# Modulation matmuls in groups of eight k tiles, and their sums turned into columns by transposes and a vector sum

## The chip, the cores and the metric

The kernel runs on one core of a Trainium2 chip. The metric is device time in microseconds (us), lower is better. It was 1266.31 us in the median of three runs (1264.38, 1266.31 and 1266.55).

## What is computed

The reference is one step of a two-layer transformer trunk on 128 context tokens and 256 latent tokens, each 2048 wide. Each layer normalizes its input and modulates it by shift, scale and gate, which are products of a condition vector with a weight matrix of 2048 x 6144:

```python
def modulate(x, cond, norm_w, ada_w, ada_b):
    m = jax.nn.silu(cond) @ ada_w + ada_b
    shift, scale, gate = jnp.split(m, 3, axis=-1)
    h = rmsnorm(x, norm_w) * (1 + scale[:, None]) + shift[:, None]
    return h, gate[:, None]
```

There are two conditions, one for the context tokens and one for the latent tokens. After the modulation, layer 0 projects h to queries, keys, values, pooling inputs and gates, runs differential attention and a pooling mixer, and projects back. Layer 1 does the same with grouped-query attention. Everything is float32. The change touches only how m is computed and handed on.

## The kernel before

All large products are 3-term products: activations and weights are each split into a high and a low part, and each tile product is three matmuls (L428, L429 and L430 of `mm3`). A weight tile is loaded by SyncE (SP) into a buffer `raw` (two buffers of 512 KB), ScalarE (ACT) makes its high part `wh` (L404), and VectorE (DVE) its low part `wl` (L406). TensorE (PE) then runs the matmuls into the PSUM tiles `mm`.

The modulation of layer 0 stands ahead of the first projections. Its shift and scale are made in nine groups of output columns (`GROUPS`): two groups of one block of 128 columns, then seven of two blocks. One group is handled by `ada_group`. For shift and then for scale it walks the 16 k tiles of the weights. Each k tile is one matmul (L486), in which the two conditions, padded to 32 columns (`cond_cols`), are the stationary operand and the weight columns are moving; with 256 columns moving, the kernel calls it 32x256. The output goes to 32 partitions of one PSUM tile, and four consecutive k tiles go to four different sets of 32 partitions, so the tile ends with four partial sums for each condition. Each float32 matmul of this kind is two records in the trace.

One item of the work list covers four k tiles. Its loads bring four k tiles of 128 columns in one transfer, or two of 256 columns, or one of 512 columns, 256 KB each, in 11 buffers named `aw` (seven) and `acc` (four). When all 16 k tiles of shift and scale are summed, ACT copies the PSUM tile to `kq` (L490), and `mod` turns rows into columns: for each block of 128 columns a matmul with the constant `sel` (L506) adds the four partial sums and leaves two columns. `set_shift` and `set_scale` (L517 and L520, on DVE) read them from PSUM and fill the tile `AB`. `make_h` then makes the modulated tiles h of that group (L291 on DVE, L294 on ACT, L296 on DVE), and the query and key projections that use these tiles can follow. A segment of the projections is listed one group after the group that completes its h tiles.

Three more groups of this kind belong to layer 1: s0 and s3 (shift) and h0 (gate). Each has 512 columns, 16 loads of 256 KB, and the first two end in `mod` too. h0 runs at the boundary between the layers, where PE also transposes the last block of x (L258) and multiplies with `ones` to spread the norm factors (L279). The rest of the modulation is done on DVE (`ada_block`) and is not touched.

A program written in this order goes to a scheduler that chooses the final order of each engine by its own estimate of times, so instructions of one item can be taken apart and spread among others. The engines run in their given order. SP issues the loads in its order and waits at each for its buffer.

## Time and profile before

| what | value |
|---|---|
| median of three runs | 1266.31 us |
| span of the profiled execution | 1264.7 us |
| runs, lowest and highest | 1264.38 and 1266.55 us |
| PE busy | 1235.3 us, 98% of the span |
| DVE busy | 920.4 us, 73% |
| ACT busy | 529.7 us, 42% |
| chain that ended last | PE 70%, DMA 4%, DVE 3% of the span |
| records of L486 | 672 |

The profiled execution's span, 1264.7 us, lies inside the range of the runs and 1.6 us under their median. A busy PE in these rows is a PE with some matmul under way. Matmuls overlap in the pipeline, so the time that one of them takes from the next is read from the distance of two starts and not from its duration.

### The profile page before, as it was taken

How to read it: one execution, taken by the hardware profiler on the slowest of the kernel's cores; microseconds unless marked ns; L12 is line 12 of the kernel's file. 1: busy time of each engine (PE TensorE's matmuls, PEld its weight loads, DVE VectorE, ACT ScalarE, POOL GpSimd, SP SyncE). 2: the span in 40 equal slices, each digit the busy share in tenths (PEclk: the TensorE clock that was granted, in tenths of full speed). 3: DMA queues.
4: the chain of work that ended last, by engine and by line, in shares of the span. 5: the costliest groups of instructions: out<-in, count | busy, mean ns of one | idle time of the engine just before them, and what ended most of it. 6: DMA issues, size and time to landing. Idle time of an engine off the chain costs nothing.

```text
span 1264.7 us, 18302 instructions
## 1 busy us (share of the span) xinstructions
PE 1235.3 (98%) x6581; PEld 1010.0 (80%) x6581; DVE 920.4 (73%) x1607; ACT 529.7 (42%) x1048; POOL 143.5 (11%) x170
## 2 busy tenths in 40 slices
PE   5999999999999999999999999999999999999998
PEld 4666678777778989987777568888889999998886
DVE  3467568699999989666998389996698565664433
ACT  5422234435445454563323344445535554462221
POOL 0000006721000101000000100332032000000000
PEclk9999999999999999999999899999999999999999
DMA  9989964787767566358777756753452332365452
GB/s 275 351 285 300 309 199 122 236 276 227 243 223 251 189 195 204 130 191 312 255 247 254 251 179 211 233 191 117 125 167 85 102 98 84 101 205 169 159 165 101
DMA packets 174398, 253.50 MB, mean 200 GB/s; under 512 B 14646, under 2 KB 86751, under 8 KB 174307
## 3 DMA queue, kind: packets, MB, share of 16 engines
q1 hardware_dynamic: 168978, 242.78, 59.8%
q0 software_dynamic: 3296, 6.35, 1.5%
q10 hardware_dynamic: 2032, 3.21, 0.7%
q8 instruction: 51, 0.84, 0.3%
q14 instruction: 41, 0.33, 0.1%
HBM read 244.39 MB, written 7.90 MB: 199 GB/s over the span
## 4 chain that ended last, share of the span: by engine, by line
PE 70%; DMA 4%; DVE 3%; issue 1%; ACT 1%; POOL 0%; SPq 0%; DVEq 0%; ACTq 0%
PE mm L428 19%; PE mm L430 19%; PE mm L429 19%; DMA raw<-even_w_out 3%; PE ax L428 1%; PE ax L430 1%; DVE acc L539 1%; PE ax L429 1%; PE ax L784 1%; DVE wl L406 1%; DMA aw<-ada_w 1%; PE ax L807 1%; PE ax L486 1%; PE ax L891 1%; PE ax L856 1%
## 5 line engine op out<-in xcount | busy, mean ns | idle before, releaser
L404 ACT CAST wh<-raw 128x1024 fp32r<-128x1024 f32 x240 | 252.2, 1051 | 446.5 <-PE mm L429 208.2
L406 DVE TENSOR_TENSOR wl<-raw,wh 128x1024 fp32r<-128x1024 f32 x240 | 295.3, 1230 | 174.0 <-ACT wh L404 173.8
L428 PE MATMUL mm<-wh,h 128*128 128x512 f32 x1024 | 404.3, 398 | 3.7 <-ACT wh L404 3.2
L429 PE MATMUL mm<-wh,h 128*128 128x512 f32 x1024 | 403.3, 394 | 0.0
L430 PE MATMUL mm<-wl,h 128*128 128x512 f32 x1024 | 393.1, 395 | 1.8 <-DVE wl L406 1.8
L539 DVE SCALAR_TENSOR_TENSOR acc<-aw,sT,acc 128x512 f32<-128x512 f32 x390 | 277.6, 747 | 1.2 <-DMA aw<-ada_w 1.1
L428 PEld LDWEIGHTS mm<-wh,h 128*128 128x128 f32 x1024 | 192.4, 188 | 59.8 <-issue 11.9
L430 PEld LDWEIGHTS mm<-wl,h 128*128 128x128 f32 x1024 | 192.5, 188 | 48.2 <-issue 6.2
L429 PEld LDWEIGHTS mm<-wh,h 128*128 128x128 f32 x1024 | 192.8, 188 | 46.9 <-issue 7.7
L428 PE MATMUL mm<-h,wh 128*128 128x384 f32 x512 | 175.8, 344 | 0.0
L429 PE MATMUL mm<-h,wl 128*128 128x384 f32 x512 | 173.7, 339 | 0.0
L430 PE MATMUL mm<-h,wh 128*128 128x384 f32 x512 | 173.6, 339 | 0.0
L428 PEld LDWEIGHTS mm<-h,wh 128*128 128x128 f32 x512 | 96.2, 188 | 6.1 <-issue 4.9
L430 PEld LDWEIGHTS mm<-h,wh 128*128 128x128 f32 x512 | 96.2, 188 | 1.8 <-issue 1.6
L429 PEld LDWEIGHTS mm<-h,wl 128*128 128x128 f32 x512 | 96.3, 188 | 1.1 <-issue 0.5
L156 POOL TENSOR_TENSOR ss<-ss,mhalf 128x12 f32<-128x12 f32 (+1 forms) x9 | 32.3, 3589 | 270.0 <-DVE ss L154 270.0
L1012 DVE TENSOR_TENSOR b<-mm,b 128x512 f32<-128x512 f32 x60 | 40.9, 688 | 29.8 <-PE mm L430 29.8
L486 PE MATMUL ax<-aw,sT 128*32 128x256 f32 (+2 forms) x444 | 54.0, 424 | 5.3 <-DMA aw<-ada_w 5.3
L702 ACT CAST r<-ax 128x256 fp32r<-128x256 f32 (+1 forms) x64 | 21.8, 354 | 30.2 <-PE ax L856 28.6
L736 ACT ACTIVATE p<-ax,ti 128x384 f32<-128x384 f32 (+1 forms) x48 | 24.3, 509 | 23.5 <-DVE ti L734 22.1
L631 POOL TENSOR_TENSOR kq<-kq,b 128x128 f32<-128x128 f32 x40 | 33.0, 857 | 8.9 <-DVE kq L620 7.3
L294 ACT ACTIVATE h<-hf,ab 128x128 fp32r<-128x128 f32 x64 | 26.2, 449 | 18.0 <-DVE hf L291 17.9
(185 smaller groups left out, 1208.3 us busy)
## 6 DMA issues: line engine op xcount, KB each, us to landing
aw<-ada_w SPq DMA_DIRECT2D x333, 256.0 KB, 4.2
raw<-even_w_in SPq DMA_DIRECT2D x96, 512.0 KB, 4.2
raw<-gqa_w_in SPq DMA_DIRECT2D x80, 512.0 KB, 3.6
raw<-even_w_out SPq DMA_DIRECT2D x32, 512.0 KB, 5.0
raw<-gqa_w_out SPq DMA_DIRECT2D x32, 512.0 KB, 3.8
acc<-ada_w SPq DMA_DIRECT2D x51, 256.0 KB, 5.7
b<-x_sample SPq DMA_DIRECT2D x16, 256.0 KB, 5.9
kq<-gates SPq DMA_DIRECT2D x16, 256.0 KB, 5.5
```

Of the source, the lines that this page charges most:

```text
L156: nc.gpsimd.tensor_tensor(out=r, in0=t, in1=self.mhalf[:, :n], op=ALU.pow)
L294: nc.scalar.activation(out=h[:, 0, c0:c1], in_=hf[:, c0:c1], func=AF.Identity, bias=ab[:, k, j:j + 1])
L404: nc.scalar.copy(out=wh, in_=raw)
L406: nc.vector.tensor_tensor(out=wl, in0=raw, in1=wh.bitcast(F32), op=ALU.subtract)
L428: mm(out, lhsT=a[0], rhs=b[0], start=start, stop=False, skip_group_check=skip)
L429: mm(out, lhsT=a[1], rhs=b[0], start=False, stop=False, skip_group_check=skip)
L430: mm(out, lhsT=a[0], rhs=b[1], start=False, stop=stop, skip_group_check=skip)
L486: nc.tensor.matmul(b[32 * i:32 * i + 32, half * nw:half * nw + nw], lhsT=self.cond_cols(k0 + i), rhs=raw[i], start=k0 == 0, stop=k0 == KT ...
L539: nc.vector.scalar_tensor_tensor(out=acc[c], in0=raw[:, i, :], scalar=s, in1=acc[c], op0=ALU.mult, op1=ALU.add)
L631: nc.gpsimd.tensor_tensor(out=t2g[:, :, qq * qd:(qq + 1) * qd], in0=q[:, :, pr * qd:(pr + 1) * qd], in1=sb.broadcast_to([P, G, qd]), op=AL ...
L736: nc.scalar.activation(out=e[:, :n], in_=s, func=AF.Exp, bias=mx[:, i:i + 1], accum_out=sm[:, i:i + 1])
L1012: nc.vector.tensor_tensor(out=r, in0=bank, in1=r, op=ALU.add)
```

## The change

An item of `ada_group` now covers eight k tiles where the group is 128 or 256 columns wide, and four as before where it is 512 wide (`ada_span`). Its matmuls are issued from the last k tile to the first. Each but the first is tied behind the PE instruction that was written just before it (`keep_in_program_order`), which fixes their order among each other and to what was written before, though other instructions can still be placed between them. `RSTD_AT` goes from 2 to 1 and stands at the same k tile. In `mod`, each block of 128 columns is transposed whole into one PSUM tile (L515 of the new kernel), and one `tensor_reduce` on DVE (L518) sums the four partial sums of each condition into a small SBUF tile, from which `set_shift` and `set_scale` read. The gate h0 still uses `sel`.

```diff
+    def ada_span(self, nw):
+        return 4 if nw == 512 else 8
...
-            for i in range(4):
-                nc.tensor.matmul(b[32 * i:32 * i + 32, half * nw:half * nw + nw], lhsT=self.cond_cols(k0 + i),
-                                 rhs=raw[i], start=k0 == 0, stop=k0 == KT - 4, skip_group_check=True)
-            if half == last and k0 == KT - 4:
+            for i in reversed(range(span)):
+                q = 32 * (i % 4)
+                mm = nc.tensor.matmul(b[q:q + 32, half * nw:half * nw + nw], lhsT=self.cond_cols(k0 + i),
+                                      rhs=raw[i], start=k0 == 0 and i >= span - 4,
+                                      stop=k0 == KT - span and i < 4, skip_group_check=True)
+                if i < span - 1:
+                    self.tc.keep_in_program_order(mm)
+            if half == last and k0 == KT - span:
...
-        ps = self.t_aux()
-        for q in range(len(parts) * nt):
-            nc.tensor.matmul(ps[:, 2 * q:2 * q + 2], lhsT=m[:, q * P:(q + 1) * P], rhs=self.sel,
-                             start=True, stop=True)
+        nq = len(parts) * nt
+        pt = self.t_aux()
+        for q in range(nq):
+            nc.tensor.transpose(out=pt[:, q * P:(q + 1) * P], in_=m[:, q * P:(q + 1) * P], identity=self.ident)
+        ps = self.t_tiny(2 * nq)
+        v = pt[:, 0:nq * P].rearrange("p (q i c) -> p q c i", q=nq, i=4)
+        nc.vector.tensor_reduce(out=ps.rearrange("p (q c) -> p q c", c=2), in_=v[:, :, 0:2, :], axis=AX.X, op=ALU.add)
```

The change moves instructions on PE. The first place is the first 256-column group, on PE before; `ax_463` is its PSUM tile, `aw` and `acc` are loaded weights, and the rows between are projection matmuls.

```order
L486 MATMUL ax_463<-acc_406,sT 32x256 x2
L428 MATMUL mm_594<-wh_506,h_374 128x512
L429 MATMUL mm_594<-wh_506,h_374 128x512
L430 MATMUL mm_594<-wl_508,h_374 128x512
L428 MATMUL mm_594<-wh_506,h_454 128x512
L429 MATMUL mm_594<-wh_506,h_454 128x512
L430 MATMUL mm_594<-wl_508,h_454 128x512
L486 MATMUL ax_463<-acc_408,sT 32x256 x2
L486 MATMUL ax_463<-aw_414,sT 32x256 x2
```

The same group on PE in the new kernel, where `ax_497` is the PSUM tile.

```order
L430 MATMUL mm_619<-wh_514,h_478 128x512
L491 MATMUL ax_497<-acc_356,sT 32x256 x2
L491 MATMUL ax_497<-acc_354,sT 32x256 x2
L491 MATMUL ax_497<-aw_352,sT 32x256 x2
L491 MATMUL ax_497<-aw_350,sT 32x256 x2
L428 MATMUL mm_620<-wh_514,h_408 128x512
```

Eight modulation matmuls now stand together where two and four stood between projection matmuls.

The second place is the end of the same group on PE before: the `sel` matmuls, then the next group's first 18 modulation matmuls, then the first matmul that reads this group's own h tile, `h_542`.

```order
L430 MATMUL mm_752<-wl_666,h_454 128x512
L506 MATMUL ax_532<-sel,kq_530 128x2 x4
L486 MATMUL ax_621<-acc_474,sT 32x256 x2
L486 MATMUL ax_621<-acc_476,sT 32x256 x2
L486 MATMUL ax_621<-aw_482,sT 32x256 x2
L486 MATMUL ax_621<-aw_484,sT 32x256 x2
L486 MATMUL ax_621<-aw_490,sT 32x256 x2
L486 MATMUL ax_621<-acc_492,sT 32x256 x2
L486 MATMUL ax_621<-acc_502,sT 32x256 x2
L486 MATMUL ax_621<-aw_504,sT 32x256 x2
L486 MATMUL ax_621<-aw_514,sT 32x256 x2
L428 MATMUL mm_877<-wh_810,h_542 128x512
```

The same place on PE in the new kernel; `h_560` is the h tile.

```order
L491 MATMUL ax_497<-acc_382,sT 32x256 x2
L429 MATMUL mm_780<-wh_674,h_478 128x512
L430 MATMUL mm_780<-wl_676,h_478 128x512
L515 MATMUL ax_548<-ident,kq_546 128x128 x4
L491 MATMUL ax_657<-aw_442,sT 32x256 x2
L491 MATMUL ax_657<-aw_440,sT 32x256 x2
L491 MATMUL ax_657<-acc_438,sT 32x256 x2
L491 MATMUL ax_657<-acc_436,sT 32x256 x2
L491 MATMUL ax_657<-aw_458,sT 32x256 x2
L428 MATMUL mm_895<-wh_813,h_560 128x512
```

The transposes stand two projection matmuls behind the group's last modulation matmul, where 20 stood before, and ten modulation matmuls now stand between them and the first use of h, where 18 stood.

The third place is the boundary of the layers on PE before: `ax_7014` belongs to the gate h0, and `b_6950`, `b_6952` and `b_6954` are the last x tiles.

```order
L486 MATMUL ax_7014<-aw_6880,sT 32x512
L258 MATMUL ax_7033<-ident,b_6950 128x128
L258 MATMUL ax_7039<-ident,b_6950 128x128
L258 MATMUL ax_7045<-ident,b_6950 128x128
L258 MATMUL ax_7033<-ident,b_6952 128x128
L258 MATMUL ax_7039<-ident,b_6952 128x128
L258 MATMUL ax_7045<-ident,b_6952 128x128
L486 MATMUL ax_7014<-aw_6882,sT 32x512
L486 MATMUL ax_7014<-aw_7295,sT 32x512
L258 MATMUL ax_7033<-ident,b_6954 128x128
```

The same boundary on PE in the new kernel.

```order
L491 MATMUL ax_7036<-aw_6884,sT 32x512
L258 MATMUL ax_7055<-ident,b_6972 128x128
L258 MATMUL ax_7061<-ident,b_6972 128x128
L258 MATMUL ax_7067<-ident,b_6972 128x128
L258 MATMUL ax_7055<-ident,b_6974 128x128
L258 MATMUL ax_7061<-ident,b_6974 128x128
L258 MATMUL ax_7067<-ident,b_6974 128x128
L491 MATMUL ax_7036<-aw_6904,sT 32x512
L491 MATMUL ax_7036<-aw_6902,sT 32x512
L491 MATMUL ax_7036<-aw_6900,sT 32x512
L491 MATMUL ax_7036<-aw_6898,sT 32x512
L258 MATMUL ax_7055<-ident,b_6976 128x128
```

Before, seven matmuls of h0 stand ahead of these transposes, and five more in pieces of two, one and two stand ahead of L279; now three whole groups of four stand there. In both kernels twelve of h0's sixteen matmuls are ahead of L279.

## Rows read from the trace of the kernel before

**Rows 1.** The page: busy us, share of the span, instructions of TensorE.
```profile
PE 1235.3 (98%) x6581; PEld 1010.0 (80%) x6581; DVE 920.4 (73%) x1607; ACT 529.7 (42%) x1048; POOL 143.5 (11%) x170
```

**Rows 2.** Stretches: length, busy us (instructions) by engine, granted clock, DMA share, GB/s.
```profile
36.00:168.00 132.00, 132.00 (x863) 86.24 (x863) 79.56 (x163) 40.59 (x63) 0.00 (x0) 1.00 0.95 313
168.00:713.00 545.00, 539.81 (x2760) 441.09 (x2759) 460.83 (x750) 237.92 (x495) 80.28 (x93) 1.00 0.67 218
```

**Rows 3.** Groups by line and shape, TensorE: count, busy us, mean ns, idle before.
```profile
L486 PE MATMUL ax<-aw,sT 128*32 128x256 f32 x268 | 30.4, 385 | 0.0
L486 PE MATMUL ax<-acc,sT 128*32 128x256 f32 x180 | 22.1, 387 | 0.0
```

**Rows 4.** Timeline of TensorE: start, us, line; one visit with two matmuls.
```profile
46.27 0.40 PE L430 MATMUL mm<-wl,h 128*128 128x512 f32 x1
46.59 0.63 PE L486 MATMUL ax<-aw,sT 128*32 128x256 f32 x4
47.15 0.50 PE L428 MATMUL mm<-wh,h 128*128 128x512 f32 x1
47.49 0.40 PE L429 MATMUL mm<-wh,h 128*128 128x512 f32 x1
```

**Rows 5.** Timeline of TensorE: one visit with six matmuls.
```profile
66.11 0.39 PE L430 MATMUL mm<-wl,h 128*128 128x512 f32 x1
66.42 0.64 PE L486 MATMUL ax<-acc,sT 128*32 128x256 f32 x8
66.88 0.60 PE L486 MATMUL ax<-aw,sT 128*32 128x256 f32 x4
67.41 0.50 PE L428 MATMUL mm<-wh,h 128*128 128x512 f32 x1
67.75 0.40 PE L429 MATMUL mm<-wh,h 128*128 128x512 f32 x1
```

**Rows 6.** Timeline of TensorE: the selector matmuls of one group of four blocks.
```profile
56.61 0.39 PE L430 MATMUL mm<-wl,h 128*128 128x512 f32 x1
56.84 0.95 PE L506 MATMUL ax<-sel,kq 128*128 128x2 f32 x8
57.72 0.64 PE L486 MATMUL ax<-acc,sT 128*32 128x256 f32 x8
```

**Rows 7.** Timeline of TensorE: two transposes of 128x128 between projection matmuls.
```profile
707.41 0.39 PE L429 MATMUL mm<-wh,h 128*128 128x512 f32 x1
707.64 0.38 PE L548 MATMUL ax<-ident,kq 128*128 128x128 f32 x2
...
708.09 0.39 PE L428 MATMUL mm<-wh,h 128*128 128x512 f32 x1
```

**Rows 8.** ScalarE's timeline: the copy of a group's sums, and its h tiles.
```profile
52.34 0.59 ACT L490 COPY kq<-ax 128x512 f32<-128x512 f32 x1 [1.53 <-PE ax L486]
53.43 1.05 ACT L404 CAST wh<-raw 128x1024 fp32r<-128x1024 f32 x1
58.84 1.60 ACT L294 ACTIVATE h<-hf,ab 128x128 fp32r<-128x128 f32 x4 [1.22 <-DVE hf L291]
```

**Rows 9.** Groups by line, VectorE: the smallest sum along the free dimension.
```profile
L272 DVE TENSOR_REDUCE ti<-ssx 128x3 f32<-128x12 f32 x2 | 0.3, 166 | 1.0 <-ACT kq L248 0.8
```

**Rows 10.** Waits of SyncE from 30 to 170 us: total us, times, longest.
```profile
SPq L379 <- PE ax L486: 27.7, 41, 2.9
SPq L368 <- DVE wl L406: 23.4, 11, 4.4
```

**Rows 11.** The DMA view from 36 to 168 us, in 40 slices of 3.3 us.
```profile
GB/s 383 357 348 368 362 348 367 333 294 275 37 122 381 329 331 360 364 364 355 310 293 365 342 296 222 206 285 355 359 357 277 211 334 359 364 350 136 282 371 385
```

**Rows 12.** Timeline of TensorE at the boundary of the layers.
```profile
719.51 2.54 PE L486 MATMUL ax<-aw,sT 128*32 128x512 f32 x4 [3.14 <-DMA aw<-ada_w]
726.34 0.91 PE L279 MATMUL ax<-p,ones 128*128 128x384 f32 x2
```

**Rows 13.** Timeline of SyncE there: start, us, line, loads.
```profile
714.73 2.35 SPq L379 DMA_DIRECT2D aw<-ada_w  x5
```

More of the change, by code (lines that the diff above doesn't have):

```diff
@@ L26 @@
 SPLIT_AHEAD = 4
-RSTD_AT = 2
+RSTD_AT = 1
 ADA_L1_SPAN = 0.6
@@ L373, in load @@
             nk = 512 // nw
-            for kk in range(k0, k0 + 4, nk):
+            for kk in range(k0, k0 + self.ada_span(nw), nk):
                 self.n_ada += 1
@@ L477, in ada_group @@
         nw = nt * P
+        span = self.ada_span(nw)
         last = len(parts) - 1
@@ L496, in ada_group @@
         for half, p in enumerate(parts):
-            for k0 in range(0, KT, 4):
+            for k0 in range(0, KT, span):
                 items.append(("ada", l, k0, p * D + k_first * P, nw,
```

## The prediction

> **What bounds the kernel now.** I read the page first: PE is busy for 98% of the span, and no other engine comes near it [rows 1]. Then I read the stretches. From 36 to 168 us, where the layer-0 modulation runs among the query and key projections, PE is never without a matmul, at the full clock of 2.4 GHz, and DMA moves 313 GB/s [rows 2]. A time saved on PE there is a time saved, if the loads keep up. Third, I read how that PE time is spent. A matmul of 512 columns takes 0.23 us from its start to the next (56.61 to 56.84) [rows 6]. The 448 records of 256-column modulation matmuls (268 + 180) carry no wait of their own [rows 3], so each visit that PE pays to them is pure PE time.
>
> A visit is a run of modulation matmuls between other work. One with two matmuls (four records, two for each) takes from 46.27 to 47.49, less two ordinary steps of 0.23, which is 0.76 us [rows 4]. One with six takes 67.75 - 66.11 - 0.46 = 1.18 us [rows 5]. So four more matmuls cost only 0.42 us: up to four that write different sets of 32 partitions run together, in what I call a round. A round costs 0.42, and entering and leaving a visit 0.76 - 0.42 = 0.34 us. A visit with half a round pays for a whole one.
>
> **The change part by part.** *Groups of eight.* I counted visits and rounds of the 256-column groups in the two programs' orders; a round ends where a set of 32 partitions comes again. Before there are 40 visits and 69 rounds, after 24 and 60. The saving is 16 x 0.34 + 9 x 0.42 = 9.2 us. The trace before has two rounds more than the order gives, where loads came apart, so 10 us is its other end. The 128-column groups go from six visits to five at 17 rounds, in a stretch where PE waits for loads anyway: 0 to 0.34, I take 0.3.
>
> *Transposes.* Four selector blocks hold PE for 57.72 - 56.84 = 0.88 us [rows 6], of which 0.1 is the way into the next visit. Two transposes take 708.09 - 707.41 - 0.46 = 0.22 us, so 0.11 each [rows 7], and four 0.45. That is 0.35 saved for each group of four blocks (0.78 less 0.45, with the way out about even; 0.25 to 0.43), and nine groups have four blocks: seven in layer 0, and s0 and s3. The sum is 3.2 us. The two 2-block groups lie in the stretch that waits for loads and count nothing.
>
> The Trainium skill speaks against this term: its page "TensorE: Matmul & The Clock Gate", section "Part 4: PE-mode transpose", gives about 275 ns for a 128x128 transpose in a kernel. By that, as an estimate from that page, four would take 1.10 us, the term would be a loss of 2.9 and the whole sum 1266.3. The trace of this kernel does not agree as far as the distance of two starts goes, which is 0.11 us.
>
> *The new sum on DVE.* The nearest row is a sum of 12 elements to three, 0.17 us [rows 9]; the other bound is a read of the whole PSUM tile, as in ACT's copy of its 512 columns, 0.59 [rows 8]. Eleven such sums on an engine that is busy 80 of 132 us cost nothing that PE sees [rows 2], except on the path from the sums to h. That path took from 57.72 (PE out of the selectors) to 58.84, where ACT starts on h, and 0.4 to the first of its four parts [rows 6, 8]: 1.5 us, now about 1.7. In most groups the order leaves PE 20 or more projection matmuls or 16 modulation matmuls to run meanwhile. In two it doesn't: eight and ten modulation matmuls stand there, two rounds and three, with entry and exit some 1.1 and 1.5 us. The first of these groups has one k tile and a shorter path of 1.4. I take 0.6 us for both waits, 0 to 1.5.
>
> *The copy on ACT.* In the first 256-column group the transposes stand two projection matmuls behind the last sum. ACT's copy takes 0.59 us, and a cast of 1.05 may lie ahead of it [rows 8]; PE has about 0.9 us of work left from the last round on. I take 0.6, from 0.2 to 1.3. Elsewhere some 20 matmuls cover it, 4.6 us.
>
> *The boundary of the layers.* Before, the seven early matmuls of h0 freed seven buffers, and SP issued five loads at once from 714.73 [rows 13]; PE then waited 3.1 us for the eighth tile and reached L279 at 726.34 [rows 12]. Now the first group frees four buffers, so the twelfth tile's load is issued only after the second group, near 721. A load in this stretch took the 4.8 us from 714.73 to 719.51 at most, so the third group, which starts with the twelfth tile, starts near 725 or 726, where it started before, and runs in one piece. I take 1 us lost, between a gain of 1 and a loss of 2.5.
>
> *Order elsewhere.* The scheduler's order shifts in small ways behind this. The visits of the 64-row matmuls (L784, L792) go from 30 to 33 and those of the 512-column modulation from 15 to 16: four visits x 0.34 = 1.4 us lost. Which waits come and go in the rest cannot be read off; PE was without a matmul for 5.2 us between 168 and 713 [rows 2], and I allow 3 us either way.
>
> *The loads.* From 36 to 168 us DMA moved 313 GB/s x 132 us = 41.3 MB [rows 2]. In the first seven slices, with no dip, it moved about 362 GB/s [rows 11]; at 350 the same bytes take 118 us. PE's share of the savings there is 9.2 + 7 x 0.35 = 11.7, so PE would want them in 120 us. The two nearly meet. What speaks for the loads: the dips [rows 11] are SP waiting for buffers, 27.7 us for modulation matmuls and 23.4 for VectorE's split [rows 10]. Both follow PE's progress and shrink when PE is faster. What speaks against: a whole group now needs four transfers landed, and 11 buffers hold under three groups. The bounds are 0, and 11.7 if DMA sets this stretch's end where it is now. I take 3, near the low end, since PE had no wait there at all.
>
> **The sum.** Gains 9.2 + 0.3 + 3.2 = 12.7; losses 0.6 + 0.6 + 1 + 1.4 + 3 = 6.6; net 6.1 us. It is made on the profiled execution, whose span is 1264.7 us; I carry the difference over to the median of 1266.3: **1260.2 us**.
>
> **The rivals.** *All of it goes through.* The loads keep up, and the boundary is even: 12.7 - 0.6 - 0.6 - 1.4 = 10.1 us, 1256, and down to 1251 with luck in the order elsewhere. For it: PE had no wait in 132 us. Against it: loads of 118 us.
>
> *The loads take the place of PE.* DMA sets the end of the stretch where it was. What is left is 0.7 for s0 and s3 less 1 and 1.4: 1268, which is no change. For it: 118 us of loads against 120. Against it: SP waited for PE, not PE for SP [rows 10].
>
> *A transpose takes longer among these matmuls* than the 0.11 us of [rows 7], and its whole record of about 0.27 is paid (0.38 less 0.11). Four take 1.1 us, the 3.2 turn into a loss of 2.9, and the time is 1266.3. Against it: two starts lie 0.11 apart. The Trainium skill's page above stands for this rival.
>
> *Slower: a group waits for its last load.* PE stands in order, so behind a group of eight that lacks one 256 KB transfer every projection matmul waits too. There are 28 such groups of 256 columns. At 350 GB/s one transfer takes 0.75 us. If each group waits for one, that is 21 us, against a net of 9.1 without the term for loads: 1266.3 + 11.9 = 1278. The deciding point is 9.1 / 28 = 0.33 us of wait for each group. Against it: before, pairs stood in a fixed order among other work, and none of their 448 records waited [rows 3].
>
> **How the numbers follow.** Forecast (1256 to 1263.7): 0.46. All goes through: 0.27. Loads take over: 0.12. Longer transposes: 0.03. Slower: 0.12. About 0.2%, 2.5 us, is what a measurement here tells from no change, so faster is 0.73, the same 0.15, slower 0.12. The range of 1251 to 1269 leaves out the slower case and the farthest of the first rival.
>
> **What would show it.** Right: 24 or so visits of 0.76 to 1.2 us in the stretch that ends now at 168 us, that stretch 8 to 12 us shorter, DMA near 340 GB/s there, transposes 0.11 us apart, and everything after shifted as it stands. Wrong: idle PE ahead of the new L491 with a load of `ada_w` as its releaser, or of L515 with ACT as its releaser, adding up to more than 5 us; L279 at the boundary more than 2.5 us later against the last out-projection matmul than before; or new idle time on PE behind 170 us that this count of visits doesn't know.

## The result and the profile after

The changed kernel takes 1272.73 us in the median of four runs (1271.52 to 1273.98), the kernel before 1265.35 (1262.64 to 1266.55). The ratio is 1.0063, with a 95% interval from 1.0046 to 1.0080: the change loses 7.4 us, and the time lies outside the range of the prediction. The profiled execution of the changed kernel took 1273.51 us, with a span of 1271.7.

I read the same views in the same order. The first line of the page of after, which answers to [rows 1]:

```profile
PE 1230.3 (97%) x6541; PEld 1008.1 (79%) x6541; DVE 920.2 (72%) x1618; ACT 530.7 (42%) x1048; POOL 140.8 (11%) x170
```

TensorE (PE) is busy 5.0 us less, and the span is 7.0 us longer: the work got smaller and the waits grew by 12. The saved work is where it was forecast. The 256-column modulation matmuls of after (L491), in the columns of [rows 3]:

```profile
L491 PE MATMUL ax<-aw,sT 128*32 128x256 f32 x268 | 25.3, 383 | 1.1 <-DMA aw<-ada_w 1.1
L491 PE MATMUL ax<-acc,sT 128*32 128x256 f32 x180 | 17.9, 386 | 2.2 <-DMA acc<-ada_w 2.1
```

30.4 + 22.1 = 52.5 us of [rows 3] have become 25.3 + 17.9 = 43.2 us. These sums are not time of PE, since the two rows run side by side in part: the whole line keeps PE busy for 38.7 us before and for 31.7 after. What the forecast was made of can be counted in the two traces: 40 visits and 69 rounds before, 24 and 60 after, as forecast. What is new stands at the end of the rows: waits for loads, where [rows 3] had 0.0. PE's timeline in after, one visit of eight matmuls and one set of transposes (start, us):

```profile
44.05 0.39 PE L430 MATMUL mm<-wl,h 128*128 128x512 f32 x1
44.37 0.64 PE L491 MATMUL ax<-acc,sT 128*32 128x256 f32 x8
44.83 0.61 PE L491 MATMUL ax<-aw,sT 128*32 128x256 f32 x8
45.37 0.50 PE L428 MATMUL mm<-wh,h 128*128 128x512 f32 x1
45.71 0.40 PE L429 MATMUL mm<-wh,h 128*128 128x512 f32 x1
...
57.77 0.66 PE L515 MATMUL ax<-ident,kq 128*128 128x128 f32 x4
58.36 0.64 PE L491 MATMUL ax<-aw,sT 128*32 128x256 f32 x8
```

The visit takes 45.71 - 44.05 - 0.46 = 1.20 us, two rounds and the way in and out, which cost 1.18 by the prediction. A price for each matmul instead of each round, 0.42 / 4 = 0.105 us, would have made it 0.76 + 6 x 0.105 = 1.39. Four transposes hold PE for 58.36 - 57.77 = 0.59 us where four selector blocks held it for 0.88 [rows 6].

To see where the time goes after that, I aligned the traces by the 4944 projection matmuls (L428 to L430), which are the same in every kernel. The table gives the start of the n-th of them (counted from 0) against its start in the kernel before, in us, for one execution of each kernel. Between two columns a gain or a loss can be placed.

| n-th projection matmul | 400 | 2100 | 2160 | 2400 | 2650 | 3640 | 3700 | last |
|---|---|---|---|---|---|---|---|---|
| its start in before | 174.5 | 610.8 | 626.8 | 689.8 | 767.5 | 989.1 | 1004.5 | 1259.7 |
| changed kernel | -5.9 | -3.7 | -0.7 | -1.7 | +3.9 | +3.8 | +7.1 | +7.1 |

The modulation stage (up to n = 400) gains 5.9 us. Then three places take it back and more: 3.0 near 613 us, 5.6 at the boundary of the layers, 3.3 at the end of layer 1's attention near 1000 us. What drifts between them makes 2.2 - 1.0 = 1.2 us lost.

**The boundary.** PE's timeline of after, to be read against [rows 12]; in brackets the wait and who ended it:

```profile
711.94 1.07 PE L491 MATMUL ax<-aw,sT 128*32 128x512 f32 x8
712.94 0.87 PE L258 MATMUL ax<-ident,b 128*128 128x128 f32 x6
716.43 1.07 PE L491 MATMUL ax<-aw,sT 128*32 128x512 f32 x8 [2.62 <-DMA aw<-ada_w]
717.43 0.65 PE L258 MATMUL ax<-ident,b 128*128 128x128 f32 x3
718.33 0.90 PE L258 MATMUL ax<-ident,b 128*128 128x128 f32 x3 [0.25 <-ACT sm L267]
723.82 1.94 PE L491 MATMUL ax<-aw,sT 128*32 128x512 f32 x8 [4.59 <-DMA aw<-ada_w]
725.68 1.65 PE L279 MATMUL ax<-p,ones 128*128 128x384 f32 x2
728.72 2.15 PE L428 MATMUL mm<-wh,h 128*128 128x512 f32 x4 [1.39 <-ACT h L294]
...
733.66 0.63 PE L428 MATMUL mm<-wh,h 128*128 128x512 f32 x1
734.09 0.63 PE L429 MATMUL mm<-wh,h 128*128 128x512 f32 x1
```

Of the three groups of four of h0 the second and the third wait for the load of their last k tile, 2.62 and 4.59 us, where before one wait of 3.14 stood [rows 12]. The load of the twelfth tile ends the longer one. From the last projection matmul of layer 0 to L279 it is now 725.68 - 711.62 = 14.06 us, before 726.34 - 713.33 = 13.01. The rest comes behind L279. From there to the first projection matmul it is 728.72 - 725.68 = 3.04 us, before 728.64 - 726.34 = 2.30. The projection matmuls that follow start 0.43 us apart instead of 0.23, which costs some 2.6 us. And one matmul of h0, which before ran in the wait for h, now makes a visit of its own among the projections, some 1.2 us. With the 1.05 us ahead of L279 these are the 5.6. The clock shows in stretches of 5 us, here of after (columns as in [rows 2], the granted clock third from the end):

```profile
720.00:725.00 5.00, 1.18 (x8) 0.20 (x8) 0.00 (x0) 0.00 (x0) 0.00 (x0) 0.50 0.91 297
725.00:730.00 5.00, 3.61 (x9) 1.47 (x6) 2.12 (x7) 2.21 (x7) 0.00 (x0) 0.50 0.82 280
730.00:735.00 5.00, 5.00 (x14) 3.89 (x13) 5.00 (x23) 2.46 (x8) 0.00 (x0) 0.52 0.03 10
```

and of before:

```profile
720.00:725.00 5.00, 5.00 (x11) 1.22 (x10) 0.68 (x3) 1.24 (x3) 0.72 (x2) 0.50 1.01 365
725.00:730.00 5.00, 4.59 (x16) 1.64 (x15) 2.20 (x7) 2.77 (x8) 0.00 (x0) 0.98 1.03 345
730.00:735.00 5.00, 5.00 (x24) 4.13 (x23) 5.00 (x23) 2.38 (x7) 0.00 (x0) 1.00 0.28 102
```

In both kernels the clock falls from 2.4 to 1.2 GHz between 715 and 720 us (granted clock 0.83 there before, 0.77 after). After, it falls behind the wait of 2.62 us already: of the six transposes that follow, the first three take 0.65 us and the next three 0.90, and only then comes the wait of 4.59. Before, PE worked through the stretch of 720 to 725 us with h0's own matmuls and transposes, and was back at the full clock when the projections began. After, it waited there, and the projections began at half the clock: 23 matmul records from 725 to 735 us in place of 40.

**Near 613 us.** VectorE (DVE) in after; L550 are multiplications of layer 1's modulation, L406 is the split of the projection weights:

```profile
609.15 2.08 DVE L550 SCALAR_TENSOR_TENSOR acc<-aw,sT,acc 128x512 f32<-128x512 f32 x3 [1.69 <-DMA aw<-ada_w]
611.15 0.69 DVE L952 TENSOR_TENSOR kq<-mm,kq 128x512 f32<-128x512 f32 x1
611.75 2.07 DVE L550 SCALAR_TENSOR_TENSOR acc<-aw,sT,acc 128x512 f32<-128x512 f32 x3
613.73 1.23 DVE L406 TENSOR_TENSOR wl<-raw,wh 128x1024 fp32r<-128x1024 f32 x1
```

DVE waits 1.69 us for a load of the modulation, and behind that wait seven other instructions still stand ahead of the split that PE needs. Before, DVE had no wait there, and PE waited 0.44 us for its split. PE in after:

```profile
615.01 0.53 PE L430 MATMUL mm<-wl,h 128*128 128x512 f32 x1 [1.86 <-DVE wl L406]
615.35 0.62 PE L428 MATMUL mm<-wh,h 128*128 128x512 f32 x1
...
618.75 0.40 PE L428 MATMUL mm<-wh,h 128*128 128x512 f32 x1
```

Behind the wait the granted clock is down. The stretch from 615 to 620 us, first after, then before (granted clock third from the end):

```profile
615.00:620.00 5.00, 4.99 (x15) 3.96 (x16) 5.00 (x8) 0.72 (x2) 0.54 (x1) 0.66 0.76 234
```

```profile
615.00:620.00 5.00, 4.56 (x23) 3.48 (x22) 5.00 (x7) 0.72 (x2) 0.54 (x1) 1.00 0.57 188
```

The eight steps from 615.35 to 618.75 take 3.40 us, where eight of 0.23 make 1.84. So of the 3.0 us lost here 1.4 are a longer wait, and 1.6 the half clock behind it. PE's order here is that of before, to the last instruction; the order on DVE is another.

**Near 1000 us.** PE in after, at the end of layer 1's attention; L658 transposes the last queries:

```profile
995.68 0.49 PE L658 MATMUL ax<-ident,kq 128*128 128x128 f32 x3
997.16 0.55 PE L658 MATMUL ax<-ident,kq 128*128 128x128 f32 x3 [0.99 <-ACT p L764]
...
1000.75 0.39 PE L428 MATMUL ax<-r,r 128*128 128x256 f32 x1 [0.78 <-ACT r L713]
...
1001.68 1.08 PE L588 MATMUL ax<-acc,ones 128*32 128x256 f32 x8
...
1003.93 0.52 PE L428 MATMUL mm<-h,wh 128*128 128x384 f32 x1
```

and the same matmuls (L647, L577) in before:

```profile
991.80 0.81 PE L647 MATMUL ax<-ident,kq 128*128 128x128 f32 x6
...
995.25 0.39 PE L428 MATMUL ax<-r,r 128*128 128x256 f32 x1 [0.59 <-ACT r L702]
...
995.90 0.64 PE L577 MATMUL ax<-acc,ones 128*32 128x256 f32 x8
...
997.15 0.34 PE L428 MATMUL mm<-h,wh 128*128 128x384 f32 x1
```

In before's order 13 projection matmuls stood right ahead of these transposes and covered the softmax on ScalarE (ACT). In the order of after they stand earlier, and PE waits in four places instead of two, 2.4 us in sum instead of 1.2. Behind these waits too the granted clock is down; first after, then before:

```profile
1000.00:1005.00 5.00, 4.25 (x22) 3.11 (x23) 3.98 (x12) 2.90 (x10) 1.45 (x4) 0.66 0.38 136
```

```profile
1000.00:1005.00 5.00, 5.00 (x34) 5.00 (x33) 0.91 (x3) 1.80 (x3) 0.00 (x0) 1.00 0.01 2
```

The same work, from the first L428 on r to the first projection matmul, takes 1003.93 - 1000.75 = 3.18 us, before 997.15 - 995.25 = 1.90. The change touches nothing there: the scheduler made another order.

### The profile page after: what moved, and what is told of

The parts are those of the page before. It is cut to its first block, busy times and chain, and to the rows that moved or that the text cites. A ratio compares the mean times of both kernels' runs of the same rounds, so it can differ in the third digit from the quotient of the medians.

```text
span 1271.7 us, 18216 instructions
## 1 busy us (share of the span) xinstructions
PE 1230.3 (97%) x6541; PEld 1008.1 (79%) x6541; DVE 920.2 (72%) x1618; ACT 530.7 (42%) x1048; POOL 140.8 (11%) x170
## 4 chain that ended last, share of the span: by engine, by line
PE 88%; DMA 6%; DVE 3%; SPq 1%; issue 1%; ACT 1%; ACTq 0%; DVEq 0%
PE mm L428 24%; PE mm L429 24%; PE mm L430 24%; PE ax L491 3%; DMA aw<-ada_w 3%; PE ax L428 2%; PE ax L430 1%; PE ax L795 1%; PE ax L429 1%; DVE acc L550 1%; SPq L379 1%; PE ax L818 1%; DMA raw<-even_w_out 1%; DMA acc<-ada_w 1%; PE ax L658 1%
## 5 line engine op out<-in xcount | busy, mean ns | idle before, releaser
L406 DVE TENSOR_TENSOR wl<-raw,wh 128x1024 fp32r<-128x1024 f32 x240 | 295.5, 1231 | 181.3 <-ACT wh L404 171.7
L428 PE MATMUL mm<-wh,h 128*128 128x512 f32 x1024 | 404.1, 399 | 6.9 <-ACT wh L404 3.5
L430 PE MATMUL mm<-wl,h 128*128 128x512 f32 x1024 | 393.1, 395 | 3.4 <-DVE wl L406 3.4
L550 DVE SCALAR_TENSOR_TENSOR acc<-aw,sT,acc 128x512 f32<-128x512 f32 x390 | 278.3, 750 | 3.6 <-DMA aw<-ada_w 3.6
L428 PEld LDWEIGHTS mm<-wh,h 128*128 128x128 f32 x1024 | 193.5, 189 | 62.3 <-issue 7.8
L430 PEld LDWEIGHTS mm<-wl,h 128*128 128x128 f32 x1024 | 193.1, 189 | 47.7 <-DVE wl L406 4.5
L428 PE MATMUL mm<-h,wh 128*128 128x384 f32 x512 | 176.0, 344 | 0.0
L430 PE MATMUL mm<-h,wh 128*128 128x384 f32 x512 | 173.1, 338 | 0.0
L428 PEld LDWEIGHTS mm<-h,wh 128*128 128x128 f32 x512 | 96.4, 188 | 5.3 <-issue 4.0
L430 PEld LDWEIGHTS mm<-h,wh 128*128 128x128 f32 x512 | 96.4, 188 | 0.8 <-issue 0.5
L156 POOL TENSOR_TENSOR ss<-ss,mhalf 128x12 f32<-128x12 f32 (+1 forms) x9 | 31.7, 3523 | 259.3 <-DVE ss L154 259.3
L491 PE MATMUL ax<-aw,sT 128*32 128x256 f32 (+2 forms) x444 | 46.8, 424 | 8.5 <-DMA aw<-ada_w 8.5
L714 DVE TENSOR_TENSOR r<-ax,r 128x256 fp32r<-128x256 f32 (+1 forms) x64 | 24.1, 393 | 15.8 <-ACT r L713 15.5
```

Source lines behind the costliest of these rows:

```text
L156: nc.gpsimd.tensor_tensor(out=r, in0=t, in1=self.mhalf[:, :n], op=ALU.pow)
L406: nc.vector.tensor_tensor(out=wl, in0=raw, in1=wh.bitcast(F32), op=ALU.subtract)
L428: mm(out, lhsT=a[0], rhs=b[0], start=start, stop=False, skip_group_check=skip)
L430: mm(out, lhsT=a[0], rhs=b[1], start=False, stop=stop, skip_group_check=skip)
L491: mm = nc.tensor.matmul(b[q:q + 32, half * nw:half * nw + nw], lhsT=self.cond_cols(k0 + i), rhs=raw[i], start=k0 == 0 and i >= span - 4, s ...
L550: nc.vector.scalar_tensor_tensor(out=acc[c], in0=raw[:, i, :], scalar=s, in1=acc[c], op0=ALU.mult, op1=ALU.add)
```

## The experiments

**Theory:** PE's saved work is real, and the loss is made at these three places, by h0's order and the scheduler's new order. **Rivals:** the new way over transposes and DVE costs more than the selector did; the groups lose in their own stage what they save, by waits for loads. All runs are given against the kernel before on the same chip, whose median was 1263.9 to 1264.9 us. The table of offsets goes on with them. Its zero is the one profiled execution of before, whose span of 1264.7 us lies some 2 us above that of a median run of that kernel, so a last column of about -2 is no difference. How far one execution can be trusted is seen where two kernels have the same order on PE. Up to n = 400 the changed kernel, e3, e8 and e11 have the same order to the last instruction, and gain 5.9, 1.5, 5.1 and 3.8 us; e1 and e7 have the same, and gain 2.2 and 5.0. In e1, e3, e8 and e11 the granted clock was 0.83 from 60 to 70 us, behind a wait for a load; in the changed kernel it was 1.00. So what the groups of eight gain in their stage is 1.5 to 5.9 us, and the 5.9 above is the best of four.

| kernel | 400 | 2100 | 2160 | 2400 | 2650 | 3640 | 3700 | last |
|---|---|---|---|---|---|---|---|---|
| e1 groups of eight, selector | -2.2 | -2.3 | +0.6 | -0.6 | +4.1 | +3.9 | +5.7 | +5.7 |
| e2 before, transposes | +2.1 | +2.5 | +4.0 | +3.3 | +4.2 | +4.2 | +4.2 | +4.2 |
| e3 changed, h0 as before | -1.5 | +0.6 | +5.2 | +4.3 | +2.2 | +1.9 | +3.7 | +3.7 |
| e4 before, h0 as changed | +0.7 | +0.1 | +0.6 | -0.1 | +3.7 | +3.6 | +8.1 | +8.1 |
| e5 changed, ascending | -1.9 | -1.0 | +2.5 | +0.2 | -1.2 | -1.2 | +0.8 | +0.8 |
| e7 e1 with h0 as before | -5.0 | -5.6 | -2.5 | -3.3 | -3.7 | -3.7 | -3.7 | -3.7 |
| e8 changed, 512 as before, 0.58 | -5.1 | -4.7 | -1.0 | -4.0 | -6.3 | -6.1 | -5.9 | -1.4 |
| e6b before, 0.58 | 0.0 | 0.0 | 0.0 | -0.2 | -0.5 | -0.5 | -0.3 | +4.2 |
| e9 changed, half loads | -13.8 | -15.7 | -14.8 | -14.5 | -13.5 | -11.2 | -6.9 | -7.1 |
| e10 before, half loads | -7.7 | -8.2 | -8.5 | -9.1 | -8.9 | -8.9 | -8.9 | -9.0 |
| e11 changed, 512 as before, 17 | -3.8 | -4.2 | -1.8 | -2.2 | -5.5 | -3.7 | -2.0 | +2.9 |
| e12 before, 17 | -0.9 | -1.6 | -1.7 | -1.2 | -3.0 | +0.2 | +1.9 | +6.2 |
| e13 all but the first groups | -6.0 | -6.0 | -3.1 | -4.8 | -5.6 | -5.6 | -5.6 | -5.7 |
| e14 e13 with selector in layer 0 | -4.8 | -4.2 | -3.3 | -2.4 | -3.6 | -3.6 | -3.6 | -3.6 |

**Each half alone.** e1 puts the selector back into the changed kernel:

```diff
-        for q in range(nq):
-            nc.tensor.transpose(out=pt[:, q * P:(q + 1) * P], in_=m[:, q * P:(q + 1) * P], identity=self.ident)
...
+            nc.tensor.matmul(ps[:, 2 * q:2 * q + 2], lhsT=m[:, q * P:(q + 1) * P], rhs=self.sel,
+                             start=True, stop=True)
```

> The changed kernel with the selector matmuls put back; groups of eight, their order and the ties stay. Theory (what TensorE saves is real and is given back by waits for loads, at the boundary of the layers and in the order elsewhere): the transposes are worth 2 to 3 us where TensorE never waits, so this is slower than the changed kernel, 1275 us. Rival 1 (the way over transposes and the vector sum costs more than the selector did): faster than the changed kernel, 1270 us or less. In both, TensorE's long wait for a load of h0 at the boundary stays, since the groups of four stay.

1273.68 us, ratio 1.0076 (1.0056 to 1.0097). That is about 1 us over the changed kernel, less than the intervals part, but not under it, and not 1270 or less: the transposes do not cost the time. e2 puts the transposes and the vector sum, and nothing else of the change, into the kernel before:

> The kernel before with transposes and the vector sum alone. Theory: 2 to 3 us under the kernel before (1265.4), so about 1262.7; four transposes hold TensorE for about 0.5 us where four selector blocks held it for 0.8 to 0.9. Rival 1 (the new path costs more than the selector): 1266 us or more. Rival 2 (the order of the rest, which the scheduler makes anew, moves the time by several us): anything from 1262 to 1270 with the modulation stage itself 2 to 3 us shorter.

1270.63 us, ratio 1.0048 (1.0036 to 1.0060): a loss of 5.8 us, and the stage itself ends 2.1 us later. The theory's time was wrong, and the first rival's time, 1266 us or more, came. Its reason did not. PE's timeline of e2 around four transposes (L507):

```profile
76.95 0.60 PE L507 MATMUL ax<-ident,kq 128*128 128x128 f32 x4
77.48 0.41 PE L486 MATMUL ax<-acc,sT 128*32 128x256 f32 x2
```

The transposes take 77.48 - 76.95 = 0.53 us, against 0.88: the saving of 0.35 for a group is there. But the scheduler, which knows the transposes by its own estimate, spread the 256-column matmuls over 50 visits and 73 rounds instead of 40 and 69. Ten visits at 0.34 us and four rounds at 0.42 are 5.1 us, more than the 2.5 that seven groups at 0.35 give. A small edit moved the order of work that it doesn't touch, and the order was worth more than the edit.

**h0 at the boundary.** e3 is the changed kernel with h0 alone ascending and without ties; e4 is the kernel before with h0 alone descending and tied.

```diff
-            for i in reversed(range(span)):
+            gate = parts[0] == 2
+            for i in (range(span) if gate else reversed(range(span))):
...
-                if i < span - 1:
+                if not gate and i < span - 1:
```

```diff
-            for i in range(4):
+            gate = parts[0] == 2
+            for i in (reversed(range(4)) if gate else range(4)):
...
+                if gate and i < 3:
+                    self.tc.keep_in_program_order(mm)
```

> The changed kernel with the gate h0 alone put back to ascending order without ties, so that seven and then two, one and two of its matmuls stand ahead of the norm factors' matmul at the boundary, as before. Theory (the groups of four there cost 4.6 us: 1 us by a later start of that matmul and the rest by a long wait for a load and matmuls at half the clock behind it): 1268 us, the wait of 4.6 us for the last load gone, granted clock from 713 to 730 us back at about 0.8. Rival (the boundary costs the same either way because the last block of x is what it waits for): 1272 to 1273 us.

> The kernel before with only h0's groups of four in descending order and tied, so that four, four and four of its matmuls stand ahead of the norm factors' matmul. Theory: the boundary of the changed kernel comes back alone, 4 to 5 us slower than before, 1270 us, with a wait of over 4 us for the twelfth load and granted clock near 0.64 behind it. Rival (what is lost there is lost by the changed times of the stages before it): 1265 to 1266 us.

e3: 1267.69 us, ratio 1.0020 (1.0006 to 1.0034), 5 us under the changed kernel. Its twelve times lie in two clusters, six from 1262.8 to 1266.4 and six from 1269.0 to 1270.8 with the profiled one among them. The mean granted clock of the first six is 0.993 to 0.997, of the others 0.990 to 0.993; where in the kernel they part no trace shows. e4: 1273.43 us, ratio 1.0065 (1.0052 to 1.0078), 8.6 us over before. PE's timeline of e4 at the boundary (L487 is h0):

```profile
725.04 1.94 PE L487 MATMUL ax<-aw,sT 128*32 128x512 f32 x8 [4.08 <-DMA aw<-ada_w]
726.91 1.65 PE L279 MATMUL ax<-p,ones 128*128 128x384 f32 x2
```

h0's order alone brings the wait of over 4 us and the half clock (granted clock 0.69 from 713 to 730 us) into a kernel whose modulation stage is untouched: +3.8 from n = 2400 to 2650 in e4, and -2.1 in e3. Both forecasts hold for the boundary, that of 4 to 5 us in e4 just about. e4 also lost 4.5 us near 1000 us, which I had not expected: its order at the end of the attention is that of the changed kernel, 13 projection matmuls early. One gate's order changed the scheduler's choice 270 us later.

**Descending or tied.** e5 issues the changed kernel's groups from the first k tile to the last, with the ties.

```diff
-            for i in reversed(range(span)):
+            for i in range(span):
```

> The changed kernel with its groups issued from the first k tile to the last, ties kept. In the program's order the groups of eight then come apart again: 43 visits of 256 columns where the changed kernel has 24, and h0 stands at the boundary in pieces of seven, two, one and two, as before. Theory (the descending order, not the tie, makes both the unbroken groups and the costly boundary): no wait of over 4 us for h0's load, no gain from visits, the wait of some 3 us near 1000 us still there; about 1266 to 1269 us. Rival (the unbroken groups themselves cost more than they save, since PE stands behind each missing load): without them 1262 us or less.

1267.61 us, ratio 1.0031 (1.0020 to 1.0042). The long wait at the boundary is gone, the stage gains 1.9 us, which is about what the transposes give, and the trace has 43 visits. Near 1000 us it still loses 2.0. So the ties alone keep no group whole; with them it is the descending order that makes both the whole groups and the costly boundary. As I read it, the first matmul of a group then waits for the load that lands last, and behind it the scheduler finds the others ready. Whether the descending order would do it without the ties, no run here shows.

**The places as before.** e7 is e1 with h0 as before, which also brings back before's order near 1000 us. e8 is the changed kernel with all 512-column groups as before and ADA_L1_SPAN at 0.58, which covers the query transposes; e6b is its control, the kernel before with that constant.

```diff
+            up = parts[0] == 2
+            for i in (range(span) if up else reversed(range(span))):
```

```diff
-ADA_L1_SPAN = 0.6
+ADA_L1_SPAN = 0.58
...
+            up = nw == 512
+            for i in (range(span) if up else reversed(range(span))):
```

> Groups of eight with selector matmuls, and h0 ascending as before. The program's order then has 21 visits and 60 rounds of 256 columns (40 and 69 before), the boundary of before, and the end of layer 1's attention (near 1000 us) in the order of before. Theory (these three places are the whole difference): 19 x 0.34 + 9 x 0.42 = 10.2 us less the 4 to 7 us of load waits that the other kernels with groups of eight show between 36 and 168 us: 3 to 6 us under the kernel before, 1259 to 1262 us. Rival (groups of eight gain nothing because the loads set the stage's end): 1264 to 1266 us.

> The changed kernel with all 512-column groups ascending and without ties, as before, and with the constant that spreads layer 1's modulation 0.58 for 0.6. The program's order has 24 visits, the boundary of before, and 15 projection matmuls ahead of the last query transposes near 1000 us, where the changed kernel has none. Theory: about 5.5 us of the modulation stage's gain stay, the 4.6 us at the boundary and the 3 us near 1000 us are gone: 1260 to 1262 us. Rival (what was lost at these places turns up elsewhere): 1265 us or more.

> The control for the one before: the kernel before with only that constant at 0.58. Its order keeps the boundary and has 15 projection matmuls ahead of the last query transposes. Theory: 1264 to 1266 us, as before, since that place was covered already. Rival (the constant itself is worth several us, and the other kernel's gain is due to it): 1262 us or less.

e7: 1264.05 us, ratio 0.9997 (0.9988 to 1.0007). e1 lost 8.8 us against its kernel before, e7 0.1, and the table shows no loss at the boundary or near 1000 us. But the 3 to 6 us under the kernel before did not come: of 5.0 in the stage 3.1 go near 613 us. The time is that of the rival, though not its reason. e8: 1265.63 us, ratio 1.0019 (1.0008 to 1.0031), not the 1260 to 1262 of the theory; e6b: 1267.53, ratio 1.0031 (1.0020 to 1.0041). The control was wrong to the other side: the constant costs 3.6 us by itself, 4.5 in the profiled execution behind n = 3700, in e8 as in e6b, and there the rival of e8 was right. Against the control e8 gains 1.9 us in the medians. e11 and e12 did the same with another constant.

```diff
-KV_ITEMS = 16
+KV_ITEMS = 17
```

> The changed kernel with the 512-column groups ascending and without ties as before, and KV_ITEMS 17 for 16, a constant that sets where the rest of layer 1's modulation begins among the projections. The order at the end of layer 1's attention then has projection matmuls before, between and behind the query transposes. Theory: the modulation stage's 5 to 6 us, with the boundary and the end of the attention as in the control: 5 us under the control, and 1259 to 1262 us if the constant alone costs nothing. Rival: within 1.5 us of the control.

> The control: the kernel before with KV_ITEMS 17. Its order at the boundary is that of before and at the end of the attention that of the kernel with both. Theory: 1262 to 1266 us, as the end of the attention was covered before too. Rival: the constant moves the time by more than 2 us by itself.

e11: 1266.72 us, ratio 1.0016 (1.0005 to 1.0027); e12: 1272.64, ratio 1.0068 (1.0055 to 1.0080). With PE's order up to L279 and at the end of the attention the same in both, the change gains 5.9 us in the medians; the constant alone loses 8.4. The two traces differ by 2.9 us at n = 400 and by 3.3 at the end; where the rest of the 5.9 comes from they do not show. So the gain of the stage can reach the end of the kernel, by 1.9 us in the medians of e8 and e6b and by 5.9 here, and a constant of the schedule moves more than the whole change.

**Loads in the stage.** e9 (from the changed kernel) and e10 (from before) halve the modulation loads of the 256-column groups and leave PE's work alone. Half of these weights are left out, so they serve to ask about the stage only; each is one execution.

```diff
+                nl = 1 if nw == 256 else nk
...
-                nc.sync.dma_start(out=raw, in_=src)
-                raws += [raw[:, i, :] for i in range(nk)]
+                nc.sync.dma_start(out=raw[:, 0:nl, :], in_=src)
+                raws += [raw[:, min(i, nl - 1), :] for i in range(nk)]
```

> The changed kernel, in which each load of a 256-column modulation tile brings one k tile instead of two and both matmuls read that one (so half of these weights are left out); the work of TensorE is the same. The program's order then has 15 visits and 57 rounds of 256 columns (24 and 60 in the changed kernel). Theory (the groups of eight lose some 5 us in this stage because they wait for whole transfers): with the loads halved the waits for aw and acc between 36 and 170 us fall from 4.4 us to under 1, and the 400th projection matmul, which starts 5.4 us earlier than before in the changed kernel, starts 12 to 15 us earlier than before: 9.7 from visits and rounds of the changed kernel, 9 x 0.34 + 3 x 0.42 = 4.3 from the further joins. Rival (something else than loads holds this stage, the copies or the h tiles): not more than 9 us earlier.

> The kernel before with the same halved loads. The program's order joins groups by itself when the loads are estimated to land early: 20 visits and 62 rounds where the kernel before has 40 and 69. Theory (the price of a visit is 0.34 us and of a round 0.42 us, whatever joins them, and the fragments of before are there because the order follows the estimated landing of the loads): the 400th projection matmul starts 20 x 0.34 + 7 x 0.42 = 9.7 us earlier than before, up to 12 with the waits at the start of the stage gone. Rival (visits cost nothing that can be had back): less than 4 us earlier.

The waits of PE from 20 to 170 us (total us, times, longest), first after, then e9 (L516 is its transpose):

```profile
PE ax L491 <- DMA acc<-ada_w: 3.2, 3, 1.4
PE mm L428 <- ACT wh L404: 2.5, 1, 2.5
PE mm L428 <- ACT h L294: 2.0, 2, 1.7
PE ax L491 <- DMA aw<-ada_w: 1.2, 2, 1.1
PE ax L515 <- ACT kq L498: 1.0, 2, 0.5
```

```profile
PE mm L429 <- ACT wh L405: 3.3, 1, 3.3
PE ax L516 <- ACT kq L499: 2.4, 2, 1.9
PE ax L492 <- DMA aw<-ada_w: 2.3, 2, 2.0
PE ax L492 <- DMA acc<-ada_w: 1.0, 1, 1.0
```

e9 starts its 400th projection matmul 13.8 us earlier than before, inside the 12 to 15 of the theory and past the rival's 9. But its waits for loads fall less than forecast, from 4.4 to 3.3 us here and from 3.2 to 2.0 between 36 and 170 us, and all waits together only from 9.9 to 9.0. Of the 7.9 us that it gains on the changed kernel 4.3 are the joins, as forecast, and some 2.7 have no account; that the sum came out is in part luck. e10 starts it 7.7 us earlier, less than 9.7, with no groups of eight in its program: where loads are estimated to land early the scheduler joins visits by itself (20 instead of 40). Only the loads differ between e10 and before, so the fragments of before are a mark of the loads as the scheduler estimates them, and halved loads alone are worth more in the stage than the change.

**All in one.** e13 keeps 512-column groups as before and the selector in the first four groups; e14 has the selector in all groups of layer 0. In both orders the boundary up to L279 and the end of the attention stand as before.

```diff
+            up = nw == 512
+            for i in (range(span) if up else reversed(range(span))):
...
+        if nt == 4 or k_first > 4:
```

```diff
-        if nt == 4 or k_first > 4:
+        if l == 1:
```

> The changed kernel with the 512-column groups ascending and without ties as before, and with the selector matmuls in the first four groups; five groups of layer 0 and s0 and s3 keep the transposes. In the program's order the boundary of the layers and the end of layer 1's attention stand as before, and there are 23 visits and 59 rounds (40 and 69 before). Theory (the loss of the changed kernel lies in the order at those places, and its stage gains): 5 to 6 us gained up to 174 us, 3 of them lost again near 613 us, 2 to 4 us under the kernel before at the end: 1260 to 1262 us. Rival (something else in the change costs time): 1264 us or more.

> The same with the selector matmuls in all groups of layer 0 and transposes in s0 and s3 only; 21 visits and 60 rounds, the other places as before. Theory: five groups x 0.35 = 1.7 us of the transposes are missing, against 2 x 0.34 - 0.42 = 0.3 us for visits and rounds: 1 to 2 us slower than the other kernel, 1262 to 1264 us. Rival (transposes cost as much as selectors): the same time.

e13: 1262.34 us, ratio 0.9985 (0.9969 to 1.0001), the lowest of all kernels that compute the whole result. It is 1.6 us under before, just short of the 2 to 4 forecast, and the interval only just reaches no change; the changed kernel is 7.4 over before. e14: 1264.24 us, ratio 1.0009 (0.9996 to 1.0022). The medians differ by 1.9 us, as forecast for the five groups of transposes that part them, though the two intervals overlap; at n = 400 the difference is 1.2. No column of e13 in the table is above zero, yet it still loses 2.9 us near 613 us.

**What stays open near 613 us.** It is not that PE brings a lead there that DVE lacks: e3 comes without a lead and loses 4.6 us, e10 comes 8.2 us ahead and loses nothing. The loss goes with DVE's order between 590 and 654 us. Where that is the order of before (before, e4, e6b, e10 and e12) at most 0.5 us are lost; in all other kernels it is another, and 0.9 to 4.6 are lost. Which instruction of it makes the load late was not tried.

## Why the prediction was wrong, point by point

- **Visits and rounds, 9.2 us: right.** Visits and rounds came out as counted, and a visit of two rounds cost 1.20 us. PE's waits from 20 to 170 us grew from 5.4 to 9.9 us and the stage still gained 5.9, so its work fell by 10.4 us, where this term, 0.3 and 7 x 0.35 made 12.0.
- **Transposes, 3.2 us: right in the price.** 0.53 to 0.59 us for four, with the way on, against 0.88; 1.9 us for five groups between the medians of e14 and e13. The rival of longer transposes fell: the starts are 0.11 us apart. The Trainium skill's 275 ns ("TensorE: Matmul & The Clock Gate", "Part 4: PE-mode transpose"), which stands there beside a figure for bf16, fits a whole record of float32 here, 0.38 - 0.11 = 0.27 us in [rows 7], but in a row of them only the last pays it.
- **Waits for h, 0.6 (0 to 1.5): too small.** 2.0 us in two waits.
- **The copy, 0.6: not there.** PE's waits for kq are 1.0 us in both kernels, all of it ahead of the 256-column groups.
- **Loads, 3 us: about right in size.** The terms of the stage made 9.2 + 0.3 + 7 x 0.35 - 0.6 - 0.6 - 3 = 7.7 us, and 5.9 came, in three more executions of the same order 5.1, 3.8 and 1.5. The waits of L491 for loads are 4.4 us, 2.6 before; 3.2 of them fall on the 28 groups of 256 columns, 0.11 each: under the 0.33 from which the slower rival decides. DMA moved 313 GB/s from 36 to 168 us, as before, and not the 340 that were to show the prediction right.
- **The boundary, 1 us (-1 to 2.5): this step failed.** Its mechanism was read rightly: four buffers instead of seven come free early, the twelfth load waits, L279 starts 1.05 us later. The failure is that I ended the sum at L279. It came to 5.6 us in all: PE, which before worked while it waited for the last tiles, now stood still, L279 and the projections behind it ran at half the clock until 734.5 us, and one matmul of h0 was left for later. e3 and e4 show that h0's order alone does it. Of the slower rival, a group that waits for its last load, the mechanism was right and the place wrong: not the 28 groups of the stage, but the second and third group of h0.
- **Order elsewhere, 1.4 us (3 either way): this step failed too.** It came to 1.2 + 3.0 + 3.3 = 7.5 us, where 1.4 lost and 0.7 gained by s0 and s3 were forecast. I took it as a count of visits. What it holds near 1000 us is cover, projection matmuls that stood ahead of a softmax: before, e2, e7, e10, e13 and e14 have one and the same order on PE from n = 3580 to 3700 and lose nothing there, after, e1, e3 and e4 have one and the same other order and lose 1.8 to 4.5 us. Near 613 us it is a late split on DVE, whose cause is open. And at both places it holds the half clock behind the wait, which I did not think of: 1.6 us near 613, 3.18 - 1.90 = 1.3 near 1000. e4 near 1000 us, e6b and e12 lost 3.6 to 8.4 us without any of the change's gain.

Of the error of 13.2 us in the profiled execution 1.8 lie in the stage, 4.6 at the boundary, and 6.8 in the order elsewhere. The last of the signs of being wrong came true, new idle time behind 170 us that the count of visits doesn't know. The sign of more than 5 us of waits of L491 and L515 did so only just, with 4.4 + 1.0, of which 3.6 had stood before.

## What to carry to other kernels

Where a scheduler orders the program by its own estimates, price a change by reading the new order at each place where PE waits or nearly waits, also far from the edit and on the other engines; a count of instructions says nothing of their cover. A group issued and tied from its last tile stayed whole here and waited for its latest load first. That gained where loads were nearly ahead, in the stage, and cost most at the boundary, where PE waited for loads already, so keep such an order out of such stretches. And follow a longer wait past its end: here the work behind it ran at half the clock, which doubled the loss near 613 us. One trace of each kernel is not enough to price a few us; the same order gave 1.5 to 5.9.

## What the hardware showed that I had not expected

How long the half clock lasts after a wait. In after PE stood still for 4.59 us up to 723.82, and from 728.72 it ran projection matmuls without a gap; they were 0.43 us apart until 734.5 and 0.23 after that, with a granted clock of 0.50 to 0.52 in all three stretches from 720 to 735 us. The same work at the full clock would have taken about half of those 5.8 us. Shorter waits did it too: the one of 1.86 us near 613 us, and those near 1000 us, at most 0.99 us each. There e1, e3, after and e4 have the same order on PE and nearly the same waits, 2.3 to 2.4 us in sum, and lose 1.8, 1.8, 3.3 and 4.5 us: the granted clock from 1000 to 1005 us was 1.00 in e1 and e3, 0.66 in after and 0.50 in e4. So waits of one length cost up to 2.7 us more by the clock behind them.
